# A grouped softmax on one core: the first tile cut into pieces of 5 and 11 groups

## The chip, the core and the metric

The kernel runs on one core of a Trainium2 chip. The core has engines with instruction queues of their own: TensorE (PE), VectorE (DVE), ScalarE (ACT), GpSimd (POOL) and SyncE (SP). They meet at semaphores. Transfers between the chip's memory (HBM) and the core's on-chip memory (SBUF, 128 partitions) are done by 16 DMA engines; SP and POOL issue the transfers here, each into a queue of its own, q1 and q0.

The metric is the device time of one execution in microseconds (us). Nine executions of the kernel before took 1324.10 to 1324.73 us, median 1324.43. The profile is of one further execution.

## The reference

```python
def reference(x):                       # x: (4, 4096, 4352) float32, normal draws
    B, N, D = x.shape
    G = 8
    Dg = D // G                         # 544
    x_g = x.reshape(B, N, G, Dg)
    x_g = x_g - x_g.max(axis=-1, keepdims=True)
    exp = np.exp(x_g)
    out = exp / exp.sum(axis=-1, keepdims=True)
    return out.reshape(B, N, D).astype(np.float32)
```

Each of the 16384 rows is split into 8 groups of 544 numbers, and each group gets its own softmax. 285.2 MB are read and as many written.

## The kernel before

**Tiles.** A tile is 256 rows: each of the 128 partitions holds two neighbouring rows, 8704 numbers or 34816 bytes that lie together in HBM, and so 16 groups. There are 64 tiles of 4.46 MB. Six buffers hold them, tile t in buffer t mod 6, and everything is done in place.

**The main path of a tile.** SP loads it (line 126). ACT takes the exponential of the whole tile in one instruction (line 73), without subtracting the maximum. DVE sums each group (line 83), takes the reciprocals of the 16 sums (line 85) and multiplies the tile by them (line 88). Then the tile is stored, by POOL (line 138) for tiles 0 to 61 and by SP (line 134) for the last two. The list `parts` (lines 62 and 63) says which instructions there are: one entry for each whole tile, and for the last tile two entries, since its two rows are loaded (line 129), exponentiated, summed and scaled apart. It is stored in one transfer.

**The check for extreme values.** Because no maximum is subtracted, DVE keeps the largest sums and reciprocals seen (`peak`, line 96, after each six tiles), tests them at the end (lines 101 to 119), and only if a test fails is everything computed again with the maximum (the code under `If_cmp`). With these inputs it isn't.

**What sets the order.** The program is written by hand, queue by queue, and each queue runs strictly in its order:
- SP: six loads at once, then for each further tile a wait until the tile that had its buffer has been stored (line 123), and its load. After all loads, the stores of tiles 62 and 63.
- POOL: for each tile a wait on `scaled` (line 137), and its store.
- ACT: the exponentials in order, each waiting for its load.
- DVE: for each entry of `parts` sum, reciprocal, scaling. The first 36 tiles run in a loop of 6 turns with 6 tiles each, the rest are written out.

So a load can be issued only when a store has landed, and after the first six the two queues are tied to each other through the six buffers.

Of the kernel before, what the change touches and what calls it, by code (L numbers as in the profile page):

```python
# [9 lines left out]
def kernel(  # L10
# [5 lines left out]
    nc = tc.nc  # L16
# [3 lines left out]
    NT = 6  # L20
    RG = R * G
# [3 lines left out]
    Dg = D // G  # L25
    nt = N // (P * R)
    LAST = 2
    TURNS = 6
    LOW, HIGH = 1e-6, 1e30
    f32 = mybir.dt.float32  # L30
    X = mybir.AxisListType.X
    Exp = mybir.ActivationFunctionType.Exp
    op = mybir.AluOpType
    xt = xf.rearrange("(t p r) d -> t p (r d)", p=P, r=R)
    ot = of.rearrange("(t p r) d -> t p (r d)", p=P, r=R)

    landed = [tc.alloc_semaphore(f"landed{b}") for b in range(NT)]
    stored = [tc.alloc_semaphore(f"stored{b}") for b in range(NT)]
    last_landed = tc.alloc_semaphore("last_landed")
    last_stored = tc.alloc_semaphore("last_stored")  # L40
    exp_done = tc.alloc_semaphore("exp_done")
    own = tc.alloc_semaphore("own")
    scaled = tc.alloc_semaphore("scaled")
# [7 lines left out]
    bufs = [ctx.enter_context(nc.sbuf_tensor(f"xt{b}", [P, R * D], f32)) for b in range(NT)]  # L51
    vals = ctx.enter_context(nc.sbuf_tensor("vals", [P, NT, 2, RG], f32))
    peak = ctx.enter_context(nc.sbuf_tensor("peak", [P, NT, 2, RG], f32))
# [5 lines left out]
    verdict = ctx.enter_context(nc.sbuf_tensor("verdict", [1, 1], mybir.dt.int32))  # L59
    found = ctx.enter_context(nc.psum_tensor("found", [1, 2], f32))  # L60

    parts = [(t, slice(0, RG)) for t in range(nt - 1)]
    parts += [(nt - 1, slice(r * G, (r + 1) * G)) for r in range(R)]

    def grouped(b):
        return bufs[b][:, :].rearrange("p (g d) -> p g d", d=Dg)

    def groups(t, g):
        return grouped(t % NT)[:, g, :]

    def scalar_exp(n):
        t, g = parts[n]
        i = nc.scalar.activation(out=groups(t, g), in_=groups(t, g), func=Exp, scale=1.0)  # L73
        if g.start == 0:
            i.wait_op(landed[t % NT], 16 * (t // NT + 1), "sem-ge")
        else:
            i.wait_op(last_landed, 16, "sem-ge")
        i.then_inc(exp_done, 1)

    def vector_scale(n, exp_at, at):  # L80
        t, g = parts[n]
        b = t % NT
        nc.vector.reduce_sum(out=vals[:, b, 0, g], in_=groups(t, g), axis=X).wait_op(  # L83
            exp_done, exp_at, "sem-ge").then_inc(own, 1)
        nc.vector.reciprocal(out=vals[:, b, 1, g], in_=vals[:, b, 0, g]).wait_op(  # L85
            own, at + 1, "sem-ge").then_inc(own, 1)
        xg = groups(t, g)
        nc.vector.tensor_tensor(  # L88
            out=xg,
            in0=xg,  # L90
            in1=vals[:, b, 1, g].unsqueeze(2).to_broadcast([P, g.stop - g.start, Dg]),
            op=op.mult,
        ).wait_op(own, at + 2, "sem-ge").then_inc(scaled, 1)

    def vector_keep(at):
        nc.vector.tensor_tensor(  # L96
            out=peak[:, :, :, :], in0=peak[:, :, :, :], in1=vals[:, :, :, :], op=op.max,
        ).wait_op(own, at, "sem-ge").then_inc(own, 1)
        nc.vector.wait_ge(own, at + 1)

    def judge(at):
# [16 lines left out]
        nc.vector.wait_ge(tested, 5)  # L118
        nc.vector.tensor_copy(out=verdict[:, :], in_=count[:, :]).then_inc(judged, 1)  # L119

    for t in range(nt):
        if t >= NT:
            nc.sync.wait_ge(stored[t % NT], 16 * (t // NT))
        tile_in = bufs[t % NT]
        if t < nt - 1:
            nc.sync.dma_start(out=tile_in[:, :], in_=xt[t]).then_inc(landed[t % NT], 16)  # L126
        else:
            for r in range(R):
                nc.sync.dma_start(
                    out=tile_in[:, r * D:(r + 1) * D], in_=xt[t, :, r * D:(r + 1) * D],  # L130
                ).then_inc(landed[t % NT] if r < R - 1 else last_landed, 16)
    for t in range(nt - LAST, nt):
        nc.sync.wait_ge(scaled, t + 1 if t < nt - 1 else len(parts))
        nc.sync.dma_start(out=ot[t], in_=bufs[t % NT][:, :]).then_inc(last_stored, 16)

    for t in range(nt - LAST):
        nc.gpsimd.wait_ge(scaled, t + 1)
        nc.gpsimd.dma_start(out=ot[t], in_=bufs[t % NT][:, :]).then_inc(stored[t % NT], 16)  # L138
    for t in range(nt - NT, nt - LAST):
        nc.gpsimd.wait_ge(stored[t % NT], 16 * (t // NT + 1))  # L140
# [4 lines left out]
    for n in range(len(parts)):  # L145
        scalar_exp(n)

    nc.vector.memset(peak[:, :, :, :], 0.0).then_inc(own, 1)  # L148
    with nc.vector.Fori(0, TURNS):  # L149
        for n in range(NT):  # L150
            vector_scale(n, n + 1, 1 + 2 * n)
        nc.vector.sem_inc(exp_done, -NT)
        vector_keep(1 + 2 * NT)
        nc.vector.sem_inc(own, -(1 + 2 * NT))
    done = 1
    for n in range(TURNS * NT, len(parts)):
        vector_scale(n, n + 1 - TURNS * NT, done)
        done += 2
        if parts[n][0] % NT == NT - 1 or n == len(parts) - 1:
            vector_keep(done)  # L160
            done += 1
    judge(done)
# [5 lines left out]
    with nc.If_cmp(regs, 2 * P, "IS_LT"):  # L168
# [3 lines left out]
        with nc.Fori(0, nt, engines=[ET.SP, ET.Activation, ET.DVE]) as t:  # L172
# [11 lines left out]
            for g in range(RG):  # L184
                i = nc.scalar.activation(
                    out=grouped(0)[:, g, :], in_=grouped(0)[:, g, :], func=Exp,
                    bias=mx[:, g:g + 1], scale=1.0, accum_out=vals[:, 0, 0, g:g + 1])
# [5 lines left out]
                out=mx[:, :], in_=grouped(0), axis=X, negate=True).then_inc(again["max"], 1)  # L193
# [6 lines left out]
                out=grouped(0), in0=grouped(0),  # L200
                in1=vals[:, 0, 1, :].unsqueeze(2).to_broadcast([P, RG, Dg]),
                op=op.mult).then_inc(again["out"], 1)
# [30 lines left out]
```

## Time and profile before

| what | value |
|---|---|
| median of nine runs | 1324.43 us |
| the profiled execution | 1324.48 us, its span 1322.7 us |
| busy: DVE, ACT, POOL, PE | 1199.7, 478.7, 33.4, 0.2 us |
| bytes moved by the DMA engines | 570.47 MB, mean 431 GB/s over the span |
| bytes in q1 (all loads, two stores) and q0 (62 stores) | 294.13 MB and 276.30 MB |
| exponential of a tile (16 groups), of half a tile | 7.457 us, 3.831 us |
| sums of a tile, of half a tile | 9.218 us, 4.680 us |
| reciprocals of a tile, of half a tile | 0.253 us, 0.203 us |
| scaling of a tile, of half a tile | 9.225 us, 4.692 us |
| a `peak` update (128 x 192) | 0.351 us, 11 times |
| longest waits | POOL for the scaling 1233.6 us, SP for stores to land 1195.0 us, ACT for loads 815.8 us, DVE for ACT 101.1 us |

Busy time counts instructions of an engine, not its waits. DVE is the busiest engine, and the DMA engines were busy in all 40 slices of the span but the beginning of the first and the end of the last. The lines "us to landing" of the profile give, for each DMA, the time from the instruction that issues it to the semaphore that says all of it has arrived; this includes the time it stands behind others in its queue. As ACT's exponential waits for nothing but its load once the pipeline runs, its start marks a load's landing, and SP's next issue marks a store's landing.

### The profile page before, as it was taken

The numbers are of one execution on the slowest core, as the hardware profiler recorded it, in microseconds if no ns is written. First come the engines' busy times: TensorE is split into PE (matmuls) and PEld (weight loads), VectorE is DVE, ScalarE is ACT, GpSimd is POOL, SyncE is SP. The second block draws the span as 40 slices with busy tenths as digits, with TensorE's granted clock in tenths as the row PEclk, the third lists the DMA queues.
The fourth block names the chain that finished last, engine by engine and source line by source line (L and its number), as shares of the span: only waits on it lengthen the run. The fifth ranks groups of instructions, "written<-read, shape, count | busy, mean of one in ns | idle before, by whom it ended". The sixth has DMA issues, their size and how long they took to land.

```text
span 1322.7 us, 513 instructions
## 1 busy us (share of the span) xinstructions
PE 0.2 (0%) x2; PEld 0.1 (0%) x2; DVE 1199.7 (91%) x213; ACT 478.7 (36%) x66; POOL 33.4 (3%) x66
## 2 busy tenths in 40 slices
PE   0000000000000000000000000000000000000000
PEld 0000000000000000000000000000000000000000
DVE  3999999999998988989889899898998988989895
ACT  4443342433424324244242342423424334243331
POOL 0000000000000000000000000000000000000000
DMA  9999999999999999999999999999999999999999
GB/s 404 421 437 429 432 438 435 424 438 438 434 425 438 437 427 433 438 435 424 438 438 433 426 438 437 426 435 437 434 426 438 436 432 430 437 436 425 437 437 389
DMA packets 18580, 570.47 MB, mean 431 GB/s; under 512 B 2064, under 2 KB 2064, under 8 KB 2064
## 3 DMA queue, kind: packets, MB, share of 16 engines
q1 hardware_dynamic: 9648, 294.13, 51.6%
q0 software_dynamic: 8928, 276.30, 48.3%
q14 instruction: 4, 0.03, 0.0%
HBM read 285.21 MB, written 285.21 MB: 431 GB/s over the span
## 4 chain that ended last, share of the span: by engine, by line
another core or an unknown queue 66%; DMA 7%; DVE 6%; SPq 1%; ACT 1%; issue 0%; PE 0%; DVEq 0%
DMA out_dram<-xt 4%; DMA xt<-in_x_dram 3%; DVE xt L88 3%; DVE vals L83 3%; SPq L126 1%; ACT xt L73 1%; DVE vals L85 0%; DVE extreme L103 0%; DVE peak L96 0%; DVE within L109 0%; PE found L113 0%; DVE count L117 0%; DVE verdict L119 0%; DVEq L149 0%
## 5 line engine op out<-in xcount | busy, mean ns | idle before, releaser
L73 ACT ACTIVATE xt<-xt 128x8704 f32<-128x8704 f32 (+1 forms) x65 | 477.4, 7345 | 815.8 <-DMA xt<-in_x_dram 815.8
L83 DVE TENSOR_REDUCE vals<-xt 128x16 f32<-128x8704 f32 (+1 forms) x65 | 590.1, 9078 | 101.9 <-ACT xt L73 101.1
L88 DVE TENSOR_TENSOR xt<-xt,vals 128x8704 f32<-128x8704 f32 (+1 forms) x65 | 590.6, 9086 | 2.2
L138 POOL DMA_DIRECT2D out_dram<-xt x62 | 33.2, 535 | 1233.6 <-DVE xt L88 1233.6
L85 DVE RECIPROCAL vals<-vals 128x16 f32<-128x16 f32 (+1 forms) x65 | 16.3, 252 | 2.2
L96 DVE TENSOR_TENSOR peak<-peak,vals 128x192 f32<-128x192 f32 x11 | 3.9, 351 | 0.0
L144 ACT ACT_TABLE_LOAD x1 | 1.3, 1283 | 0.9 <-PEq L217 0.9
L148 DVE MEMSET peak<- 128x192 f32 x1 | 0.2, 218 | 1.1 <-PEq L217 1.1
L117 DVE TENSOR_REDUCE count<-found 1x1 f32<-1x2 f32 x1 | 0.1, 147 | 0.3 <-PE found L113 0.3
L103 DVE TENSOR_REDUCE extreme<-peak 128x2 f32<-128x192 f32 x1 | 0.3, 348 | 0.0
L113 PE MATMUL found<-within,one 128*1 128x2 f32 x2 | 0.2, 164 | 1307.0 <-DVE within L109 1307.0
L109 DVE TENSOR_SCALAR within<-extreme 128x1 f32<-128x1 f32 x2 | 0.2, 148 | 0.0
L119 DVE CAST verdict<-count 1x1 int32<-1x1 f32 x1 | 0.1, 142 | 0.0
L113 PEld LDWEIGHTS found<-within,one 128*1 128x1 f32 x2 | 0.1, 80 | 1307.0 <-DVE within L109 1307.0
L217 POOL MEMSET const-float32-0.0<- 128x1 f32 x1 | 0.1, 100 | 0.3 <-issue 0.3
L217 POOL MEMSET const-bfloat16-1.0<- 128x1 bf16 x1 | 0.1, 103 | 0.0
L217 POOL MEMSET const-float32-1.0<- 128x1 f32 x1 | 0.1, 100 | 0.0
L217 POOL MEMSET const-uint8-127<- 128x1 uint8 x1 | 0.1, 100 | 0.0
L102 DVE MEMSET one<- 128x1 f32 x1 | 0.1, 59 | 0.0
## 6 DMA issues: line engine op xcount, KB each, us to landing
xt<-in_x_dram SPq DMA_DIRECT2D x63, 4352.0 KB, 41.9
out_dram<-xt POOLq DMA_DIRECT2D x62, 4352.0 KB, 54.3
out_dram<-xt SPq DMA_DIRECT2D x2, 4352.0 KB, 19.5
xt<-in_x_dram SPq DMA_DIRECT2D x2, 2176.0 KB, 44.9
```

The source lines that it names most:

```text
L73: i = nc.scalar.activation(out=groups(t, g), in_=groups(t, g), func=Exp, scale=1.0)
L83: nc.vector.reduce_sum(out=vals[:, b, 0, g], in_=groups(t, g), axis=X).wait_op(exp_done, exp_at, "sem-ge").then_inc(own, 1)
L85: nc.vector.reciprocal(out=vals[:, b, 1, g], in_=vals[:, b, 0, g]).wait_op(own, at + 1, "sem-ge").then_inc(own, 1)
L88: nc.vector.tensor_tensor(out=xg, in0=xg, in1=vals[:, b, 1, g].unsqueeze(2).to_broadcast([P, g.stop - g.start, Dg]), op=op.mult,).wait_op( ...
L96: nc.vector.tensor_tensor(out=peak[:, :, :, :], in0=peak[:, :, :, :], in1=vals[:, :, :, :], op=op.max,).wait_op(own, at, "sem-ge").then_in ...
L103: nc.vector.tensor_reduce(out=extreme[:, :], in_=peak[:, :, :, :].rearrange("p b k g -> p k b g"), axis=mybir.AxisListType.XY, op=op.max,) ...
L109: nc.vector.tensor_scalar(out=within[:, k:k + 1], in0=extreme[:, k:k + 1], scalar1=most, scalar2=None, op0=op.is_le).then_inc(tested, 1)
L113: nc.tensor.matmul(out=found[:, :], lhsT=one[:, :], rhs=within[:, :], start=True, stop=True).then_inc(counted, 1)
L126: nc.sync.dma_start(out=tile_in[:, :], in_=xt[t]).then_inc(landed[t % NT], 16)
L138: nc.gpsimd.dma_start(out=ot[t], in_=bufs[t % NT][:, :]).then_inc(stored[t % NT], 16)
L144: nc.scalar.preload_act_table(Exp)
L217: nc = _bacc.Bacc("TRN2", target_bir_lowering=False, num_devices=1)
```

## The change

Tile 0 gets two entries in `parts`: its first 5 groups (2720 numbers in each partition, 10880 bytes) and the other 11 (5984 numbers, 23936 bytes). Each piece has a load, an exponential, sums, reciprocals, a scaling and a store. Tile 6, the next user of buffer 0, waits for both stores. The other tiles are as before, but their number in the list is one higher, so the counts waited for shift by one. DVE works on the two pieces ahead of its loop, with a `peak` update of buffer 0 of its own, and the loop then runs over tiles 1 to 36 instead of 0 to 35.

```diff
+    FIRST = 5
...
+    first_landed = tc.alloc_semaphore("first_landed")
+    first_stored = tc.alloc_semaphore("first_stored")
...
-    parts = [(t, slice(0, RG)) for t in range(nt - 1)]
+    parts = [(0, slice(0, FIRST)), (0, slice(FIRST, RG))]
+    parts += [(t, slice(0, RG)) for t in range(1, nt - 1)]
...
-        if g.start == 0:
+        if n == 0:
+            i.wait_op(first_landed, 16, "sem-ge")
+        elif g.start == 0 or t == 0:
             i.wait_op(landed[t % NT], 16 * (t // NT + 1), "sem-ge")
...
-    def vector_keep(at):
+    def vector_keep(at, b=slice(0, NT)):
         nc.vector.tensor_tensor(
-            out=peak[:, :, :, :], in0=peak[:, :, :, :], in1=vals[:, :, :, :], op=op.max,
+            out=peak[:, b, :, :], in0=peak[:, b, :, :], in1=vals[:, b, :, :], op=op.max,
...
+    cut = FIRST * Dg
     for t in range(nt):
+        if t == NT:
+            nc.sync.wait_ge(first_stored, 16)
         if t >= NT:
             nc.sync.wait_ge(stored[t % NT], 16 * (t // NT))
         tile_in = bufs[t % NT]
-        if t < nt - 1:
+        if t == 0:
+            nc.sync.dma_start(out=tile_in[:, :cut], in_=xt[t, :, :cut]).then_inc(first_landed, 16)
+            nc.sync.dma_start(out=tile_in[:, cut:], in_=xt[t, :, cut:]).then_inc(landed[t % NT], 16)
+        elif t < nt - 1:
...
-        nc.sync.wait_ge(scaled, t + 1 if t < nt - 1 else len(parts))
+        nc.sync.wait_ge(scaled, t + 2 if t < nt - 1 else len(parts))
...
-    for t in range(nt - LAST):
-        nc.gpsimd.wait_ge(scaled, t + 1)
+    nc.gpsimd.wait_ge(scaled, 1)
+    nc.gpsimd.dma_start(out=ot[0, :, :cut], in_=bufs[0][:, :cut]).then_inc(first_stored, 16)
+    nc.gpsimd.wait_ge(scaled, 2)
+    nc.gpsimd.dma_start(out=ot[0, :, cut:], in_=bufs[0][:, cut:]).then_inc(stored[0], 16)
+    for t in range(1, nt - LAST):
+        nc.gpsimd.wait_ge(scaled, t + 2)
         nc.gpsimd.dma_start(out=ot[t], in_=bufs[t % NT][:, :]).then_inc(stored[t % NT], 16)
...
+    vector_scale(0, 1, 1)
+    vector_scale(1, 2, 3)
+    vector_keep(5, slice(0, 1))
     with nc.vector.Fori(0, TURNS):
-        for n in range(NT):
-            vector_scale(n, n + 1, 1 + 2 * n)
+        for n in range(2, 2 + NT):
+            vector_scale(n, n + 1, 2 + 2 * n)
         nc.vector.sem_inc(exp_done, -NT)
-        vector_keep(1 + 2 * NT)
+        vector_keep(6 + 2 * NT)
         nc.vector.sem_inc(own, -(1 + 2 * NT))
-    done = 1
-    for n in range(TURNS * NT, len(parts)):
+    done = 6
+    for n in range(2 + TURNS * NT, len(parts)):
         vector_scale(n, n + 1 - TURNS * NT, done)
         done += 2
-        if parts[n][0] % NT == NT - 1 or n == len(parts) - 1:
+        if parts[n][0] % NT == 0 or n == len(parts) - 1:
             vector_keep(done)
```

## The prediction

> **What bounds the kernel now.** I read the shares of the engines first, then the DMA rate by stretch, then the issues and landings of the DMAs, and last the two ends of the timeline. VectorE is busy for 91% of the span, which looks like the bound, but the rate by stretch says otherwise (columns: stretch and its length, busy time of PE, PEld, DVE, ACT, POOL with counts, clock, DMA share, GB/s):
>
> ```profile
> 2.00:40.00 38.00, 0.00 (x0) 0.00 (x0) 18.60 (x3) 20.63 (x4) 0.00 (x0) 1.00 0.99 424
> 40.00:46.00 6.00, 0.00 (x0) 0.00 (x0) 6.00 (x2) 1.93 (x1) 0.67 (x1) 1.00 0.97 354
> 46.00:66.00 20.00, 0.00 (x0) 0.00 (x0) 19.93 (x4) 7.46 (x1) 0.53 (x1) 1.00 1.03 446
> ...
> 300.00:1238.00 938.00, 0.00 (x0) 0.00 (x0) 857.42 (x147) 336.38 (x46) 24.52 (x46) 1.00 1.00 433
> ```
>
> The DMA engines are full from about 2 us to the end, loads alone or loads beside stores, and 433 GB/s is all they give. 570.5 MB at that rate is 1317 us of the 1322.7. So the change can only matter where it makes the DMA engines idle, or stops an idleness. Two queues share them: loads on SP's, stores on POOL's. The issue rows (count, KB each, median us from issue to landing):
>
> ```profile
> xt<-in_x_dram SPq DMA_DIRECT2D x63, 4352.0 KB, 41.9
> out_dram<-xt POOLq DMA_DIRECT2D x62, 4352.0 KB, 54.3
> ```
>
> One tile in and one out is 8.91 MB, 20.57 us at the full rate, and that is the distance between SP's issues in the chain of waits (354.32, 374.88, 395.45). So a load spends 41.9/20.57 = 2.04 tile times in its queue and a store 2.64. The first number matters below: how far loads run ahead of stores. Now the start and the end of the timeline (start, duration, engine, line):
>
> ```profile
> 13.85 7.46 ACT L73 ACTIVATE xt<-xt 128x8704 f32<-128x8704 f32 x1 [11.65 <-DMA xt<-in_x_dram]
> 21.33 9.22 DVE L83 TENSOR_REDUCE vals<-xt 128x16 f32<-128x8704 f32 x1 [20.04 <-ACT xt L73]
> 24.16 7.46 ACT L73 ACTIVATE xt<-xt 128x8704 f32<-128x8704 f32 x1 [2.86 <-DMA xt<-in_x_dram]
> ...
> 30.88 9.22 DVE L88 TENSOR_TENSOR xt<-xt,vals 128x8704 f32<-128x8704 f32 x1
> ...
> 40.41 0.67 POOL L138 DMA_DIRECT2D out_dram<-xt  x1 [39.95 <-DVE xt L88]
> ...
> 66.38 0.33 SPq L126 DMA_DIRECT2D xt<-in_x_dram  x1
> 67.14 7.46 ACT L73 ACTIVATE xt<-xt 128x8704 f32<-128x8704 f32 x1 [13.12 <-DMA xt<-in_x_dram]
> ...
> 1260.68 7.46 ACT L73 ACTIVATE xt<-xt 128x8704 f32<-128x8704 f32 x1 [13.10 <-DMA xt<-in_x_dram]
> ...
> 1301.37 4.69 DVE L88 TENSOR_TENSOR xt<-xt,vals 128x4352 f32<-128x4352 f32 x1
> ```
>
> An ACT start is a load's landing: tile 0 at 13.8, tile 1 10.31 us later, so a load alone takes 10.31 us. SP's issue at 66.38 is the landing of tile 0's store, which POOL issued at 40.41. For line 134, the last two stores, the answer by line is:
>
> ```profile
> L134 SPq DMA_DIRECT2D out_dram<-xt x2: 343/344/344, 1287.0 to 1306.1; - x2
> ...
> DMA to landing us min/median/max: 15.2/19.5/23.9
> ```
>
> Tile 62's store lands at 1287.0 + 23.9 = 1310.9, the last at 1306.1 + 15.2 = 1321.3, 10.4 later: it stood behind the other and the DMA engines never ran dry. How nearly? SP's first load had nothing ahead of it and took 12.9 us from issue to landing (0.90 to 13.82, the least of line 126). Alone, the last store would have landed at 1306.1 + 12.9 = 1319.0. **The slack at the end is 2.3 us**: if the last scaling comes later than that, the end moves with it.
>
> What sets the last scaling? Tile 62's load lands at 1260.7; its exponential, sums and scaling (7.46, 9.22, 9.22), then those of the two halves of tile 63 follow with VectorE full, up to 1306.1: 45.4 us that nothing shortens. So the end is the later of "all bytes moved" and "tile 62 landed + 45.4 + 12.9".
>
> **The lead of the loads.** While both queues hold work, they move the same bytes (a load and a store each take 20.57 us a tile), so loads moved minus stores moved stays what it was when the store queue became continuous. At 66.36 before, one store was done, and load 4 was 0.76 us from landing: 4.96 loads. The lead is 3.96 tiles. Tile 62's load is the 63rd; it lands when 126 minus the lead tiles have moved in all. Each tile of lead lost lands it 10.28 us later, with the same bytes moved. That is what to ask of the change.
>
> **The change, part by part.** From rows of whole and half tiles the price per group and the fixed part follow: exponential 7.457 and 3.831, so 0.453 a group and 0.205 fixed; sum 9.218 and 4.680, so 0.567 and 0.142; scaling 9.225 and 4.692, so 0.567 and 0.159; reciprocal 0.253 and 0.203.
>
> Piece one (5 groups): landed at 13.85 - 10.31 x 11/16 = 6.76; exponential 2.47 to 9.23; sum 2.98, reciprocal 0.18, scaling 2.99, with their gaps to 15.5; POOL issues its store at 15.85, the 0.3 later that it is now. Before, nothing was stored until 40.41.
>
> Piece two (11 groups): exponential 13.85 to 19.04; sum 6.38, reciprocal 0.22, scaling 6.39, to 32.15; store issued at 32.46. The new peak instruction and its wait (0.35 and 0.42, from L96 and the wait after it) end at 32.9.
>
> Tile 1: its load shares with piece one's store and lands 1 to 2 us later, at 25.2 to 26.0; exponential to 33.5; sums to scaling 18.77 (21.33 to 40.10 now); done at 52.0, store issued at about 52.3, against 59.08 now.
>
> Store landings: tile 0's took 66.36 - 40.41 = 25.95, of which sharing explains 20.57; 5.4 is overhead of a POOL store that finds its queue empty. A piece's rows are shorter, and the queues seem to alternate row by row (tile 63's two loads of half rows beside stores of whole rows landed 15.4 us apart, 1276.1 and 1291.6, where equal bytes would give 10.3: a third of the rate). So piece one shares with a whole load: 1.39 + 4.46 MB, 13.5 us; piece two 3.06 + 4.46 MB, 17.4 us. Piece one lands at 15.85 + 5.4 + 13.5 = 34.8, piece two at 32.46 + 5.4 + 17.4 = 55.2. Tile 1's store, issued at 52.3, lands at 52.3 + 5.4 + 20.57 = 78.3 if it pays the overhead whole. It is issued before piece two has landed, so some may be hidden; with the 2.6 us of overhead that SP's first load shows (12.9 - 10.3) it lands at 75.5. I take 77.0, between them, as half of the overhead is likely covered. From there POOL has the next store ready in time: VectorE gives a tile each 18.7 us (59.08, 77.75, 96.42 now), and stores drain one in 20.57.
>
> The ledger at 77.0: before, 5.96 tiles had moved by 66.36. 10.64 us more at 10.28 a tile is 1.03: 7.00 moved, 2 of them stores, 5.00 loads. **The lead is 3.00, 0.96 less.** The store queue took DMA time that loads had for themselves, and SP can't give it back, since a new load is issued only when a store lands. Tile 62 then lands 0.96 x 10.28 = 9.9 us later. Of that the slack at the end hides 2.3; the rest is a dry DMA between the end of tile 62's store and the last one. **The sum is +7.6 us.**
>
> Ends: lead lost 0.84 (78.3) to 1.11 tiles (75.5), 8.6 to 11.4 us. Slack: nearest row 2.3; if the last store had no overhead (10.3 alone) 4.9; if it paid the 5.4 of a POOL store, nothing. So +3.7 to +11.4. Stretch 40 to 46 shows that a queue's start also cost rate: 354 and then 446 over 26 us make 0.5 us lost. Now it may happen at three stores; two more losses, each counted in the lead and in the bytes, are 0 to +2 us, taken as 0.
>
> Nothing else costs. SP issues one more load (0.33 to 0.53 us) while 6.8 us of work wait; ACT gets one more fixed 0.2 us beside 816 us of idleness; VectorE some 1.3 us, already counted in tile 1's time; POOL one more issue of 0.53 us, idle 1233 us. SP's new wait for piece one's store stands before tile 6's load and all behind it; it is over at 34.8, and the old wait for tile 0 (now piece two) at 55.2 ends last. The thresholds of POOL's and SP's later waits shift by one with the count and wait for the same work. The peak updates move by one tile, none to the end.
>
> The Trainium skill, DMA: Bandwidth & Descriptors, section on the anatomy of one DMA on the GpSimd path, gives a store a fixed 2.0 us plus its bytes at 436 GB/s and wants large transfers. By that fixed part charged in line for two more transfers, the loss would be an estimated 4 us; this trace has the six first loads issued in 2.98 us and landing 10.31 apart, so in a filled queue the fixed part is hidden, and 5.4, not 2.0, is what an empty store queue cost.
>
> **The rivals.** (1) The lead comes back: if the store queue ran empty for some microseconds after tile 1, loads would have the full rate and each such microsecond makes up one of the 9.9. From 5 us of emptiness on the result is no longer slower than the bound of 0.2% (2.65 us, about what a measurement of this kernel tells from no change). For it: VectorE's next tile is ready at 71.0, and with 5.4 overhead only 0.6 us ahead of 77.0. Against: the margin grows by 1.9 us a tile, and load 2 lands near 40, long before. Time 1324.4 to 1327. (2) Faster, as DMA work starts earlier on the store side: against it is 433 GB/s in all stretches; at most the 0.5 to 1 us lost at 40 to 46 goes, 1323.5. A gain of over 0.2% would need more rate. (3) Dearer: three restarts of the queue with their loss of rate, and the last store paying the whole 5.4: +11.4 + 2, up to 1338. That the change doesn't do what it says is out: VectorE and ACT hold the split instructions first in their order.
>
> **How the numbers follow.** The profiled run took 1324.48 us around its span of 1322.7, at the median of 1324.43. 1324.4 + 7.6 = 1332.0. Chances: lead lost as worked out 0.80, (1) 0.12, (2) 0.02, (3) 0.06. Slower is 0.86, same 0.12 and faster 0.02. The range takes 1328.1 to 1335.9 of the likeliest, a part of (1) below and of (3) above: 1327 to 1336.5.
>
> **What would show it.** Stores issued at 15.9, 32.5 and 52.3; SP's first waiting load at 55; the median load 61.7 us to landing (41.9 + 0.96 x 20.57) and the store 34.5, their sum still 96.2; tile 62's exponential at about 1270.6; at the end a stretch of some 5 us without DMA, and the last store landing in 13 us rather than 15.2. Wrong would be: loads still near 42 us (the lead was kept), or no dry stretch before the last store.

## The result and the profile after

The changed kernel took 1342.88 us in the median of ten executions, against 1324.43 us before. It is slower, and it is unsteady: 1334.48, 1334.55, 1334.85 and 1335.10 us, then 1342.57, 1343.19 and 1345.36, then 1386.01, 1391.82 and 1394.31. The kernel before kept within 1324.09 to 1325.22 in 30 (in the 48 taken beside the experiments all but two were below 1325.5; those were 1326.33 and 1330.77). The ratio to before is 1.0106, interval 1.0092 to 1.012, and it leaves out the executions more than 1.5% above the fastest; with them the median is 1.4% up. Four more executions of the changed kernel are on record, outside this median: 1335.30, 1347.24, 1405.87 and 1406.59 us.

So there are two things to explain: the 8 to 11 us that every execution pays, and up to some 70 us more that most pay in part. Two profiles show them apart. The one taken with the result (1405.87 us) is an expensive execution. The same kernel was profiled again later, in an execution of 1332.83 us (the first experiment), a cheap one. Its issues (count, KB each, median us to landing), of the load and the store rows that were 41.9 and 54.3 before:

```profile
xt<-in_x_dram SPq DMA_DIRECT2D x62, 4352.0 KB, 60.7
out_dram<-xt POOLq DMA_DIRECT2D x61, 4352.0 KB, 36.4
```

The sum is 97.1 (96.2 before): a load spends 18.8 us longer in its queue and a store 17.9 less. A load's 60.7 us are 2.95 tile times, so with six buffers the loads lead by 3.05 tiles. The start and the end of its timeline:

```profile
15.70 0.67 POOL L149 DMA_DIRECT2D out_dram<-xt  x1 [15.24 <-DVE xt L94]
...
32.30 0.53 POOL L151 DMA_DIRECT2D out_dram<-xt  x1 [15.94 <-DVE xt L94]
...
52.47 0.53 POOL L154 DMA_DIRECT2D out_dram<-xt  x1 [19.64 <-DVE xt L94]
...
54.53 0.33 SPq L138 DMA_DIRECT2D xt<-in_x_dram  x1
77.32 0.33 SPq L138 DMA_DIRECT2D xt<-in_x_dram  x1
...
1271.76 7.46 ACT L77 ACTIVATE xt<-xt 128x8704 f32<-128x8704 f32 x1 [13.11 <-DMA xt<-in_x_dram]
...
1312.44 4.69 DVE L94 TENSOR_TENSOR xt<-xt,vals 128x4352 f32<-128x4352 f32 x1
```

Stores start 25 us earlier than before, tile 0 is stored at 54.5 and tile 1 at 77.3, and yet tile 62 lands 11.1 us later (1271.76, was 1260.68), and with it the last scaling (1312.44, was 1301.37). The rate by stretch shows what that does (last columns: DMA share, GB/s), and the answer for the last two stores gives their landing:

```profile
300.00:1240.00 940.00, 0.00 (x0) 0.00 (x0) 853.83 (x144) 343.01 (x46) 24.45 (x46) 1.00 1.00 433
1300.00:1308.00 8.00, 0.00 (x0) 0.00 (x0) 7.93 (x4) 3.83 (x1) 0.00 (x0) 1.00 1.05 455
1308.00:1312.00 4.00, 0.00 (x0) 0.00 (x0) 4.00 (x1) 0.00 (x0) 0.00 (x0) 1.00 0.73 313
1312.00:1316.00 4.00, 0.00 (x0) 0.00 (x0) 3.93 (x3) 0.00 (x0) 0.00 (x0) 1.00 0.00 0
1316.00:1320.00 4.00, 0.19 (x2) 0.09 (x2) 2.25 (x8) 0.00 (x0) 0.00 (x0) 1.00 0.65 279
```

```profile
L146 SPq DMA_DIRECT2D out_dram<-xt x2: 343/344/344, 1298.0 to 1317.2; - x2
...
DMA to landing us min/median/max: 12.4/13.6/14.8
```

433 GB/s until the end, then a hole of 5.5 us (1312.5 to 1318.0, by the packets) while VectorE finishes tile 63, then the last store alone, 12.4 us after its issue instead of 15.2. The last store no longer waits for the DMA engines; they wait for it. 11.1 us later and 2.8 less of waiting make 8.3; the span grew by 8.4 (1331.1 against 1322.7).

In the expensive execution the middle itself is slower:

```profile
xt<-in_x_dram SPq DMA_DIRECT2D x62, 4352.0 KB, 64.5
out_dram<-xt POOLq DMA_DIRECT2D x61, 4352.0 KB, 38.2
```

```profile
300.00:1240.00 940.00, 0.00 (x0) 0.00 (x0) 819.65 (x139) 322.04 (x44) 22.92 (x43) 1.00 1.00 414
1300.00:1340.00 40.00, 0.00 (x0) 0.00 (x0) 34.93 (x6) 14.91 (x2) 1.07 (x2) 1.00 0.92 393
1340.00:1380.00 40.00, 0.00 (x0) 0.00 (x0) 38.00 (x9) 15.12 (x3) 0.53 (x1) 1.00 0.55 236
```

A share of 1.00 at 414 GB/s says that all engines are occupied and move less; 236 GB/s at a share of 0.55 says that near the end many of the 16 stand idle while others still work. The trace keeps, for each transfer, the moment at which each engine reports its part done. For some loads of this execution, the delay of each behind the first engine:

```
load landed at   14 engines       the last two
     55.5        0.0 to 0.3       0.3, 0.4
     78.7        0.0 to 0.4       4.1, 4.4
    103.6        0.0 to 0.3       8.0, 8.7
    128.4        0.0 to 0.5      12.9, 12.9
    178.6        0.0 to 0.7      20.7, 21.9
    334.5        0.0 to 3.6      44.6, 47.0
```

Two engines fall behind from 60 us on, by 4.3 us a tile. The delay stops at 47 us: a load's 64.5 us less 47 is under a tile time, so the other engines have next to no issued loads left, and all go at the pace of those two, 21.5 us a tile (8.91 MB at 414 GB/s). At the end tile 62's load lands 45.6 us, and the first half of tile 63's 49.9 us, after the first engine has done its part. Stringing the packets of one engine together (each starts where the last ended) shows how it begins. L is a row of a load, S of a store, each 34816 bytes, with its start and, where it isn't 1.29 us, its duration:

```
one of the 14   L 56.1  S 57.4  L 58.7  S 60.0  L 61.3  S 62.5         L 63.8  S 65.1         L 66.4
one of the two  L 55.1  S 56.4  L 57.7  S 59.0  L 60.3  S 61.6 (1.79)  L 63.3  S 64.6 (2.00)  L 66.6
```

Each engine takes load and store rows in turn, one row each. The two are one row out of step with the others, and not only since tile 1's store: they already took the first row of piece two's store one load row later, at 37.7 us, where the other 14 took it at 36.1 to 36.4. From 61.6 us on some of their store rows take up to 2.1 us.

That is how it begins, not how it stays. Between 60 and 250 us, 82 store rows and 23 load rows of this execution take over 1.6 us (1.86 and 1.71 in the mean). Between 300 and 1240 us it is 815 of 5556 load rows (1.92 in the mean) and 28 of 5620 store rows (none over 1.65): once the delay has settled, the lost time lies mostly in load rows. Stringing the packets from 600 to 625 us shows it on both sides: on most engines one load row in each tile takes 1.7 to 2.6 us, and two engines have store rows of 1.3 to 1.6 us in between.

How much each execution loses by this can be added up. Of all whole rows that start between 100 and 1200 us, take the time beyond 1.29 us, and divide the sum by the 16 engines:

```
profile                       us lost per engine
changed, expensive                44.0
last store split (below)          36.5
one store for tile 0 (below)      21.3
changed, cheap                     1.8
five buffers (below)               0.55
before                             0.05
```

In the stores from ACT it is 0.2 and 0.4, in the longer hold of loads 0.3, and in the other kernels below under 0.1. So the cheap execution of the changed kernel has a little of the same loss: by 1200 us it had moved 116.16 tiles' worth of bytes, where the kernel before had moved 116.33, which is 1.7 us at 10.28 us each.

### The profile page after: what moved, and what is told of

The parts are those of the page before. It is cut to its first block, busy times and chain, and to the rows that moved or that the text cites. A ratio compares the mean times of both kernels' runs of the same rounds, so it can differ in the third digit from the quotient of the medians.

```text
span 1404.1 us, 521 instructions
## 1 busy us (share of the span) xinstructions
PE 0.2 (0%) x2; PEld 0.1 (0%) x2; DVE 1201.3 (86%) x217; ACT 478.9 (34%) x67; POOL 33.9 (2%) x67
## 4 chain that ended last, share of the span: by engine, by line
another core or an unknown queue 61%; ACT 32%; DVE 3%; DMA 3%; issue 0%; SPq 0%; PE 0%; POOLq 0%
ACT xt L77 32%; DMA xt<-in_x_dram 3%; DVE xt L94 1%; DVE vals L89 1%; DVE vals L91 0%; SPq L138 0%; SPq L136 0%; SPq L135 0%; DVE extreme L109 0%; DVE peak L102 0%; DVE within L115 0%; PE found L119 0%; DVE count L123 0%; DVE verdict L125 0%
## 5 line engine op out<-in xcount | busy, mean ns | idle before, releaser
L77 ACT ACTIVATE xt<-xt 128x8704 f32<-128x8704 f32 (+2 forms) x66 | 477.6, 7237 | 899.7 <-DMA xt<-in_x_dram 899.7
L89 DVE TENSOR_REDUCE vals<-xt 128x16 f32<-128x8704 f32 (+2 forms) x66 | 590.3, 8945 | 184.4 <-ACT xt L77 184.4
L94 DVE TENSOR_TENSOR xt<-xt,vals 128x8704 f32<-128x8704 f32 (+2 forms) x66 | 590.7, 8950 | 2.3
L91 DVE RECIPROCAL vals<-vals 128x16 f32<-128x16 f32 (+2 forms) x66 | 16.5, 250 | 2.3
L102 DVE TENSOR_TENSOR peak<-peak,vals 128x192 f32<-128x192 f32 (+1 forms) x12 | 4.0, 338 | 0.0
## 6 DMA issues: line engine op xcount, KB each, us to landing
xt<-in_x_dram SPq DMA_DIRECT2D x62, 4352.0 KB, 64.5
xt<-in_x_dram SPq DMA_DIRECT2D x1, 2992.0 KB, 12.2
```

The lines of the kernel that those rows point to most:

```text
L94: nc.vector.tensor_tensor(out=xg, in0=xg, in1=vals[:, b, 1, g].unsqueeze(2).to_broadcast([P, g.stop - g.start, Dg]), op=op.mult,).wait_op( ...
L102: nc.vector.tensor_tensor(out=peak[:, b, :, :], in0=peak[:, b, :, :], in1=vals[:, b, :, :], op=op.max,).wait_op(own, at, "sem-ge").then_in ...
```

## The experiments

Two theories stood at the start: the lead (the prediction's), and rows of unequal length, which the pieces bring and which might disturb the engines whatever the lead. All times below are those of each kernel beside the kernel before on the same chip (median 1324.43 to 1324.60 there). Lines that a diff leaves out are marked with dots.

**The changed kernel again.** No edit.

> The changed kernel once more. Lead theory: a load stays about 62 to 65 us in its queue and a store 34 to 38; where the 16 DMA engines stay in step the time is near 1334.5, about 10 us over before, with a dry stretch before the last store; where two of them fall behind, as in the first profile, it is 8 to 70 us more. Theory of the engines out of step alone (the unequal rows disturb them, the lead costs nothing): with all engines in step the time is 1324 to 1326.

Measured: 1332.83, 1347.28, 1388.34 and 1396.74 us. The cheap execution is the one shown above: all engines in step within 3 us, a load at 60.7 us, and still 8.3 us over before. So it is not engines out of step alone.

**Hold tile 1's store.**

```diff
     for t in range(1, nt - LAST):
         nc.gpsimd.wait_ge(scaled, t + 2)
+        if t == 1:
+            nc.gpsimd.wait_ge(landed[4], 16)
```

> The changed kernel, but POOL holds tile 1's store until load 4 has landed, so the store queue stands empty from about 55 to 66 us and the loads get the whole rate. Lead theory: at tile 1's store landing (about 92) 8.4 tiles have moved, 2 of them stores, a lead of 4.4 against 3.96 before; a load takes about 32 to 38 us in its queue, a store 58 to 64; 1324.4 to 1326, though all pieces and their rows are as in the changed kernel. Theory of the unequal rows: the pieces are still there, so 1334 or more.

Measured: 1324.75 us, ten executions from 1324.35 to 1325.56, ratio 1.0002 (0.9993 to 1.0012). The pieces, their early stores and their odd rows are all there, one wait is added, and the whole loss is gone. POOL issues tile 1's store 14 us later, and the issues read:

```profile
66.47 0.53 POOL L156 DMA_DIRECT2D out_dram<-xt  x1 [33.64 <-DMA xt<-in_x_dram]
71.10 0.53 POOL L156 DMA_DIRECT2D out_dram<-xt  x1 [4.09 <-DVE xt L94]
```

```profile
xt<-in_x_dram SPq DMA_DIRECT2D x62, 4352.0 KB, 33.4
out_dram<-xt POOLq DMA_DIRECT2D x61, 4352.0 KB, 63.3
```

A lead of 6 - 33.4/20.57 = 4.4 tiles, as worked out beforehand. This refutes the theory of the unequal rows and shows the lead as the cause of what every execution pays.

**One store for tile 0.** Loads, exponentials, sums and scalings stay in pieces; the store is whole.

```diff
-    nc.gpsimd.wait_ge(scaled, 1)
-    nc.gpsimd.dma_start(out=ot[0, :, :cut], ...).then_inc(first_stored, 16)
     nc.gpsimd.wait_ge(scaled, 2)
-    nc.gpsimd.dma_start(out=ot[0, :, cut:], ...).then_inc(stored[0], 16)
+    nc.gpsimd.dma_start(out=ot[0], in_=bufs[0][:, :]).then_inc(stored[0], 16)
```

> The changed kernel with tile 0's two loads, exponentials, sums and scalings, but one store of whole rows, issued at 32.4 us when both pieces are scaled. Lead theory: it lands 8 us before that of the kernel before, 0.77 tile less lead, 7.9 us, of which 2.3 or a little more are hidden at the end: 1329 to 1331; a load takes about 58 us, a store 38. Theory of the unequal rows: no unequal stores, so at most 1326.

Measured: 1346.49, 1350.37, 1358.94 and 1360.77 us, ratio 1.021 (1.016 to 1.026). Slower, as the lead says, but by far more than it says: a load takes 60.1 us, a store 39.6, and in the middle (300 to 1240 us) the rate is 424 GB/s. There are no unequal store rows here, and engines fall behind all the same, up to 9.7 us by the end. Between 60 and 250 us not one store row here takes over 1.6 us, and 68 load rows do, so long store rows are no necessary part of it.

**The same, held.** The whole store of tile 0 also waits for load 3.

```diff
     nc.gpsimd.wait_ge(scaled, 2)
+    nc.gpsimd.wait_ge(landed[3], 16)
```

> As the kernel with one store, but that store is held until load 3 has landed (about 44.8 us; before it was issued at 40.4). Lead theory: lead 0.4 tile more than before; a load takes about 33 us, a store 63; 1324 to 1325. Theory of the unequal rows (here the first tile's loads): 1324 to 1326 too.

Measured: 1324.88 us, ten executions from 1324.37 to 1325.65, ratio 1.0003 (0.9994 to 1.0013); a load 32.3 us, a store 64.5. An earlier VectorE with a store that is not earlier costs nothing and gains nothing.

**Five buffers.** `NT = 5` in the changed kernel. The lead is set at the start and stays; the loads' queue gets shorter by one tile.

> The changed kernel with five tile buffers instead of six. The lead of the loads is set at the start and stays about 3.0 tiles, but with one buffer less a load waits one tile time less in its queue: about 41 us, a store about 36. With all DMA engines in step: 1331 to 1334, as in the changed kernel. If engines fall behind because the store queue is short (36 us), they do so here too, 1335 to 1400; if because the load queue is long (61 us), they don't, and all times are 1331 to 1334.

Measured: 1331.32, 1335.35, 1344.69 and 1384.64 us; a load 40.0 us, a store 36.1. The cheap execution costs what it did with six buffers, so the load's 60 us are no cost in themselves; the lead is. By the other times, engines seem to fall behind with a short load queue too; the profile is of the cheap execution.

**Hold the second piece.** Its store also waits for load 2.

```diff
     nc.gpsimd.wait_ge(scaled, 2)
+    nc.gpsimd.wait_ge(landed[2], 16)
```

> The changed kernel, but the store of tile 0's second piece is held until load 2 has landed (40 us, not 32.3). Lead theory: the piece's store lands near 62.7, tile 1's at 83.3, when 7.6 tiles have moved, 2 of them stores: lead 3.6, 0.35 less than before, 3.6 us, of which the slack at the end hides 2.3 to 2.9; a load takes about 49 us, a store 47; 1325 to 1327 with the engines in step. If the step is lost by a short store queue, it should be lost less or not at all here.

Measured: 1326.71 to 1327.57 us, median 1327.22, with no expensive execution in four. The lead was 3.4 (a load 54.0 us) rather than 3.6: the piece's store was issued at 38.5, and load 2 had landed a little sooner than I took. (3.96 - 3.37) x 10.28 = 6.1, less 2.8 of slack, is 3.3; measured 2.8, 0.2 above the range.

**Split the last store.** Tile 63's store in two halves, each as soon as it is scaled.

```diff
-        nc.sync.wait_ge(scaled, t + 2 if t < nt - 1 else len(parts))
-        nc.sync.dma_start(out=ot[t], in_=bufs[t % NT][:, :]).then_inc(last_stored, 16)
+        if t < nt - 1:
...
+        else:
+            for r in range(R):
+                nc.sync.wait_ge(scaled, len(parts) - R + 1 + r)
+                nc.sync.dma_start(out=ot[t, :, r * D:(r + 1) * D], ...).then_inc(last_stored, 16)
...
```

> The changed kernel with tile 63's store in two halves, the first as soon as its half is scaled. Lead theory: the loss sits in the dry stretch before the last store, so with the engines in step the last half lands 7.8 us after its issue, not 12.4: 1327.5 to 1329 against 1332.8. If the loss were not at the end (lower rate throughout), no gain: 1332 or more.

Measured: 1330.44, 1381.68, 1386.93 and 1395.11 us. The profile fell on an expensive execution (six engines late this time, the other ten in step), so the end can't be read from it. 1330.44 is below all 14 executions of the changed kernel, but it is one, and 1.4 us over what was expected at most: inconclusive.

**Stores from ACT's hardware queue.** The stores of tiles 0 to 61 are issued by ACT, each behind the next tile's exponential, not by POOL. Run twice.

```diff
...
     for n in range(len(parts)):
         scalar_exp(n)
+        if n > 0:
+            act_store(n - 1)   # wait for scaled, then nc.scalar.dma_start as POOL had it
```

> The changed kernel with the stores of tiles 0 to 61 issued by ACT on a hardware queue, each behind the next tile's exponential. Overhead of an empty store queue 2.6 us instead of 5.4: tile 1's store lands near 75.5, lead 2.85, 1.1 less than before: 1332.5 to 1335 with the engines in step; a load takes about 64 us, a store 34. If engines fall behind because of POOL's software queue, all times are in that range; if because of the short store queue whoever issues, they scatter up to 1400.

> Stores of the changed kernel from ACT's hardware queue, once more with more executions. If POOL's software queue is needed for engines to fall behind: 1330 to 1336 throughout; if the short store queue is enough, some of the executions are at 1340 to 1400.

Measured: 1330.49 to 1330.61 three times and 1336.08; then 1330.62, 1330.65, 1330.84, 1334.44 and 1334.86. Nine executions, the same lead as in the changed kernel (a load 60.1 and 60.7 us), none over 1336.1, where the changed kernel had nine of 14 at 1342 or more. The steady cost is the lead's, 6.1 us, 2 us under the first range, as the lead came out 0.2 longer than the 2.85 expected; no great scatter was seen. The edit changes the kind of queue and the engine that issues together (the first three stores leave within 0.3 us of the same times), so which of the two matters is not shown.

**Hold the loads of the kernel before.** Now without any piece: tile 0 is whole, POOL stores as ever, and the lead is cut from the other side.

```diff
     for t in range(nt):
         if t >= NT:
             nc.sync.wait_ge(stored[t % NT], 16 * (t // NT))
+        if t == 3:
+            nc.sync.wait_ge(scaled, 1)
```

> The kernel before, whole tile 0, but SP issues load 3 and those behind it only when tile 0 is scaled (40.1 us), so the DMA engines are idle from 34 to about 42 us. Lead theory: the loads restart shortly before the stores, the lead is about 3.3 tiles, 0.7 to 0.75 less, 7.5 us, of which 2.3 to 2.9 hidden; with 8 us of idleness: 1336 to 1339; a load takes about 57 us. If the scatter of the changed kernel comes from the short lead alone, times here scatter too, 1336 to 1400; if it takes several restarts of the store queue under load, they don't.

Measured: 1336.55 to 1336.88 us, ratio 1.0092 (1.0076 to 1.0107), no scatter. Two holes in the rate, one made by the wait and one, a thousand microseconds later, by the lead:

```profile
34.00:38.00 4.00, 0.00 (x0) 0.00 (x0) 4.00 (x1) 3.46 (x1) 0.00 (x0) 1.00 0.00 0
38.00:42.00 4.00, 0.00 (x0) 0.00 (x0) 4.00 (x2) 4.00 (x1) 0.67 (x1) 1.00 0.42 113
...
1316.00:1320.00 4.00, 0.00 (x0) 0.00 (x0) 3.93 (x3) 0.00 (x0) 0.00 (x0) 1.00 0.45 192
1320.00:1324.00 4.00, 0.19 (x2) 0.09 (x2) 2.16 (x8) 0.00 (x0) 0.00 (x0) 1.00 0.65 279
```

A load takes 56.6 us and a store 40.2, a lead of 6 - 56.6/20.57 = 3.25 tiles: (3.96 - 3.25) x 10.28 = 7.3, less 2.8, is 4.5 us from the lead. The wait itself costs the bytes that did not move: by 80 us 29.5 MB against 33.4 before (0 to 30 at 400 GB/s and 30 to 80 at 350, against 406 and 425), 9.1 us at 433 GB/s. Together 13.6; measured 12.2. So the rule of the lead holds, within 1.4 us, in a kernel that has no piece at all, and in these four executions a short lead does not bring the scatter by itself.

**Eleven groups first, then five.** `FIRST = 11` in the changed kernel.

```diff
-    FIRST = 5
+    FIRST = 11
```

> The changed kernel with the first piece 11 groups and the second 5. By the ledger: first store issued at 28.9, landed 51.7; second issued at 35.1, behind it, landed 65.2; tile 1's issued at 54.5, behind that, landed 85.8, when 7.85 tiles have moved, 2 stores: lead 3.85, 0.1 less than before; a load takes about 44 us, a store 52. The slack at the end hides it: 1324.3 to 1325.5, no scatter.

Measured: 1325.89 us, ten executions from 1325.68 to 1326.29, ratio 1.001 (1.0 to 1.0019). The stores are issued at 29.23, 35.37 and 54.35, a load takes 43.8 us and a store 53.2: a lead of 3.87 (3.85 was forecast), and no scatter. By the lead nothing should be lost (0.9 us, less than the slack), and there is no dry stretch at the end; yet it is 1.35 us over, and 0.4 above the range. One engine is a row (1.3 us) behind the others at the end of this profile, which would be enough; it is one profile, so this small rest stays open.

**Eight and eight.** `FIRST = 8`.

```diff
-    FIRST = 5
+    FIRST = 8
```

> The changed kernel with two pieces of 8 groups. By the ledger: first store issued at 22.6, landed 43.4; second issued at 32.3, landed 58.8; tile 1's issued at 52.1, early enough to stand behind it, landed 79.4: lead 3.23, 0.73 less than before, 7.5 us, 2.3 to 2.9 hidden: 1329 to 1330 in step; a load takes about 57 us, a store 39. The store queue is never empty after its first start: if restarts under load put engines out of step, no scatter; if the short store queue does, scatter up to 1400.

Measured: 1327.85, 1327.93, 1332.86 and 1334.72 us, ratio 1.0054 (1.0035 to 1.0074). Stores issued at 22.53, 32.08 and 51.06; a load 56.6 us, a store 40.2, so a lead of 3.25 (3.23 was forecast). 4.5 us by the lead, 3.4 in the two cheap executions, 1 us under the range. The other two pay 5 to 7 us more: a scatter, but a small one, between what the two theories of its cause had said.

**Hold the loads of the kernel before for longer.** As in the hold of loads above, but the wait is on the third exponential.

```diff
         if t == 3:
-            nc.sync.wait_ge(scaled, 1)
+            nc.sync.wait_ge(exp_done, 3)
```

> The kernel before, whole tile 0, with load 3 and those behind it held until the exponential of tile 2 is done (41.95 us), 1.8 us longer than with the wait for tile 0's scaling (40.1). Lead theory: 1.8 us more of idleness and 0.18 tile less lead, so 3.7 us more than 1336.7: 1340.0 to 1340.8; a load takes about 60.3 us, a store 36.5 to 38.5. If engines fall behind as soon as a store's time falls under about 40 us (so far the large scatter stood at 36.1 to 39.6, none at 40.2 and over), some executions are at 1345 to 1420, though there is one start of the store queue and no piece; if it takes the pieces or several restarts, all are within 1 us of one another.

Measured: 1342.10, 1342.26, 1342.59 and 1343.11 us, ratio 1.0132 (1.0115 to 1.0149). The lead came out shorter than meant:

```profile
xt<-in_x_dram SPq DMA_DIRECT2D x63, 4352.0 KB, 65.8
out_dram<-xt POOLq DMA_DIRECT2D x62, 4352.0 KB, 31.0
```

6 - 65.8/20.57 is 2.80. The reason is in the rate where the store starts. POOL issues it at 40.47, SP its held loads from 41.95:

```profile
38.00:42.00 4.00, 0.00 (x0) 0.00 (x0) 4.00 (x2) 3.97 (x1) 0.67 (x1) 1.00 0.32 139
```

139 GB/s over 4 us are 0.56 MB, one row of 34816 bytes on each of the 16 engines, and no held load was issued yet. In half-microsecond stretches all of these rows fall into one (1114 GB/s, as a row counts where it starts):

```profile
41.50:42.00 0.50, 0.00 (x0) 0.00 (x0) 0.50 (x1) 0.47 (x1) 0.00 (x0) 1.00 2.58 1114
```

So on idle engines the store's first rows started 1.0 to 1.5 us after its issue. In the kernel before, where loads filled the engines, tile 0's store was issued at 40.41 and its first rows started between 44.9 and 46.4, 4.5 to 6.0 us after. The price: by 80 us 29.4 MB instead of 33.4, 9.3 us, and 11.9 - 2.8 = 9.1 from the lead; 18.4 in all, measured 17.8 (1342.42 in the median against 1324.60, 1.6 above the range). And there is no scatter in four executions, although a store here spends the shortest time of all kernels in its queue. That speaks against the theory that a store's time in the queue below some bound (the large scatter stood at 36.1 to 39.6 us) is enough for engines to fall behind.

**The first hold of loads, with stores from ACT.**

```diff
+        if t == 3:
+            nc.sync.wait_ge(scaled, 1)
...
     for n in range(len(parts)):
         scalar_exp(n)
+        if 0 < n <= nt - LAST:
+            nc.scalar.wait_ge(scaled, n)
+            nc.scalar.dma_start(out=ot[n - 1], ...)   # as POOL had it
```

> The kernel before with load 3 and those behind it held until tile 0 is scaled (40.1 us) and the stores of tiles 0 to 61 issued by ACT on a hardware queue, which starts some 3 us sooner than POOL's. Lead theory: lead about 3.05, a load about 60 us, a store 37; 8 us of idleness and 9.5 us of lead less 2.5 hidden: 1338 to 1341. If the short store queue alone lets engines fall behind, large scatter up to 1420; if POOL's software queue is needed too, scatter of at most 6 us.

Measured: 1338.71, 1338.75, 1338.78 and 1339.06 us, ratio 1.0106 (1.0089 to 1.0123), no scatter. A load 61.5 us, a lead of 3.01: 9.8 - 2.8 = 7.0, and 7.8 us of bytes not moved by 80 us; 14.8, measured 14.2. Under the same hold ACT's store gets going sooner than POOL's did (first rows 3.6 to 4.0 us after its issue, where POOL's took 6.2 to 7.0; a lead 0.24 shorter), and the end is 2.0 us later for it.

**All together.** The lead is the number of buffers less a load's time to landing over 20.57; the cost by it is 10.28 x (3.96 - lead) - 2.8, not below nothing, plus the time of bytes not moved at the start; measured is the cheap executions' time, or the median where there was no scatter, over the kernel before beside it (1324.43 to 1324.60).

```
kernel                        lead   by the lead  idle  measured  spread of all
hold tile 1's store           4.38       0          0      0.2        1.2
one store, held               4.43       0          0      0.4        1.3
eleven and five               3.87       0          0      1.4        0.6
hold the second piece         3.37       3.3        0      2.8        0.9
eight and eight               3.25       4.5        0      3.4        6.9
five buffers                  3.06       6.5        0      6.9       53.3
changed, stores from ACT      3.08/3.05  6.2/6.6    0      6.1/6.3    5.6/4.2
changed, again                3.05       6.6        0      8.3       63.9
hold loads, no pieces         3.25       4.5        9.1   12.2        0.3
hold loads, ACT               3.01       7.0        7.8   14.2        0.4
hold loads longer             2.80       9.1        9.3   17.8        1.0
```

(One store for tile 0 is left out, as it had no cheap execution, and the split last store, as its end is another.) Eleven kernels with leads from 2.8 to 4.4, pieces or none, POOL's queue or ACT's, are within 1.7 us of that sum, and giving the lead back (the first line) gives the time back. That settles where the 6 to 7 us come from. The largest difference, 1.7 us in the changed kernel, is the lengthening of its rows (1.8 us per engine). It is one execution, though: the four cheap ones taken with the result are 10.1 to 10.7 us over before, 3.5 to 4.1 more than the lead explains, and none of them was profiled.

The scatter is settled in part. Where it came, three things stood together, POOL's queue, tile 0's store started while loads fill the engines, and a lead that stays short: the changed kernel, one store for tile 0, five buffers and the split last store, to 1344 us and more, and in small with eight and eight. Without POOL's queue it was at most 5.6 us in nine executions; with the lead given back, at most 1.3 in twenty; with loads held until about the time of the first store, at most 1.0 in twelve. The three are not enough: the hold of the second piece has them all, at a lead of 3.37, and kept within 0.9 in four. What puts two engines, or six, a row out of step, and why rows then take longer than 1.29 us, the runs do not show. In the cheap profile of the changed kernel four engines are also a row apart from the other 12, at a cost of 1.8 us, and in the kernel before one is, at next to none, so being out of step is not enough.

## Why the prediction was wrong

The median was 1342.88 against a forecast of 1332.0 and a range up to 1336.5. Its steps one by one, by the cheap execution where nothing else is said:

- **Start.** Stores issued at 15.70, 32.30 and 52.47; 15.85, 32.46 and 52.3 were worked out. The prices per group held.
- **Landings.** Piece one's store landed at 34.1 (34.8), piece two's at 54.4 (55.2), tile 1's at 77.3 (77.0). Beyond its bytes a store took 4.9, 4.7 and 4.3 us; 5.4 twice and half hidden the third time had been taken. The row-by-row sharing, which had been inferred from two half loads, is directly visible in the packets.
- **Lead.** 3.05 against 3.00. A load 60.7 us (61.7), a store 36.4 (34.5). The rival in which the lead comes back did not happen; forced by one wait on tile 1's store, it does what was said of it.
- **Tile 62** 11.1 us later (9.9). By the measured lead it would be 0.91 x 10.28 = 9.4; the other 1.7 is the lengthening of rows through the whole execution (1.8 us per engine). It is within the 0 to 2 us set aside for the queue's restarts and then taken as 0, but it did not arise at the restarts: by 100 us as many bytes had moved as before (9.38 and 9.37 tiles).
- **Slack** 2.8 (2.3), the last store 12.4 us rather than 15.2. **Net** 8.3 (7.6), and 1332.83 us (1332.0). That these lie so close is partly luck: the lead's own part came out 1.0 us under the forecast (6.6), and the lengthened rows, which the sum did not have, filled the gap. The dry stretch is there, 5.5 us for the 5 expected.
- **The failed step** is "433 GB/s is all they give", with "Nothing else costs". The sum took the 16 engines as one pipe that, once full, always gives the same rate. It gave 414 GB/s at a share of 1.00 in the first profile, because rows of 1.29 us were lengthened by 44 us per engine between 100 and 1200 us: first on two engines that fell behind, then on all, held to the pace of those two. By their times nine of 14 executions pay for that (the ten of the median and the four of the first experiment), some 10 to 64 us on top of the 8; they make the median. What starts it stays open. No term and no rival held it: the dearest rival counted three restarts at a loss of rate of up to 2 us and stopped at 1338.
- **Slower** was right, and the lost lead was one reason for it in both profiles (a load's time 60.7 and 64.5 us); in most executions the larger part of the time has another, which the prediction did not have.

The trace of before could not have given the price: after the one start of its store queue it shows 433 GB/s for a thousand microseconds. But the change starts that queue up to three times under full loads, where the trace has no row, and 0 to 2 us, taken from the one start, was no bound for what can follow.

## What to carry to other kernels

Where loads and stores share full DMA engines and a fixed set of buffers, a store started earlier takes its time from the loads' head start, and in none of these kernels was that head start rebuilt by itself; it comes back as idle DMA at the end, where the last load still has all its computing ahead of it. Read the head start from the median times to landing (buffers less load time over tile time), compare it with the slack of the last store, and if an early piece is wanted, hold the next store until the loads are ahead again. Run such a kernel ten times, and look for stretches where the DMA share is 1.00 and the rate is below its usual: here that meant that single engines had fallen behind.

## What was not expected of the hardware

- Single DMA engines fell behind the others by 4.3 us a tile, with single store rows of up to 2.1 us against 1.29 for 34816 bytes, and from a delay of 47 us on held all 16 to 414 GB/s (300 to 1240 us), while every engine counts as busy. The Trainium skill, DMA: Bandwidth & Descriptors, section Latency and other measured facts, says that two of the 16 engines are usually slower than the rest and puts it down, as a guess, to the descriptor rings of POOL's queue. That fits the part of POOL's queue here; it does not fit that it was two engines in one profile, six in another, and none in the kernel before, which uses the same queue. The trace does not number the engines.
- Two queues share an engine row by row, one load row and one store row of 34816 bytes in turn (1.29 us each). The same page, section Queues, rings and completion order, has an engine drain a whole packet of some 9 to 17 descriptors before it turns to another queue; here it is one row, and in the kernel before half rows beside whole ones got a third of the rate (tile 63's two loads landed 15.4 us apart).
- A store from POOL started its rows 1.0 to 1.5 us after its issue on idle engines (the longer hold of loads), and 4.5 to 6.0 us after it where loads filled them (before); there a store with an empty queue took 4.3 to 5.4 us beyond its bytes.
